# A held-back half tile of matrix products, cut into two chains of 256 columns around the end of a kernel

## The chip, the core and the metric

The kernel runs on one core of a Trainium2 chip. A core has a matrix engine (PE, whose weight loads the profile keeps apart as PEld), a vector engine (DVE), a scalar engine for activations and copies (ACT), a general engine (POOL) and a queue engine that issues transfers (SP). The metric is the device time of one execution in microseconds. Before the change it is 301.92 us, the median of three runs (301.86 to 302.01).

## The reference

```python
x: [16, 512, 1024]   w1, w2: [1024, 768]     # float32
y1 = np.matmul(x, w1)
y2 = np.matmul(x, w2)
return (np.tanh(y1) * y2).astype(np.float32)
```

Flattened, x has 8192 rows: 64 tiles of 128 rows. Each tile needs 768 columns of y1 and 768 of y2, over an inner length of 1024 (8 slices of 128).

## The kernel before

Inputs are cast to float16, sums are kept in float32. The 1536 columns of both weights are three blocks of 512: "a" (the first 512 of w1), "b" (the first 512 of w2) and "g" (the last 256 of w1 beside the last 256 of w2).

The first four row tiles (HEAD = 4) are "plain": for each block a chain of 8 matmuls adds up in one of the 8 PSUM banks (`plain`, `mm`, line 426), then ACT takes the tanh (`plain_tanh`, line 429) and DVE multiplies (`plain_mul`, line 433). The other 60 tiles go in 20 triples, numbered 0 to 19. A triple's 3x3 block product is computed by a fast scheme with 15 products p0 to p14 in place of 18: sums of x blocks (`x_sum`, line 417, DVE) times sums of weight blocks, each product 4 matmuls of 128x512 (`product`, line 442, PE), with copies of partial results (`c_copy`, line 446, ACT) and additions between banks (`c_add`, line 452, DVE). The list C_OPS names every step with what it needs. The steps that the change and the prediction touch are:

- p11, copy63, p0: p0 adds onto the bank of p11 after copy63 has read it.
- t0: the tanh of the bank that p0 finishes; add60: an addition that reads that bank and writes the bank in which p4 then continues; copy60 follows p4.
- p5, add52, seed16, p3: add52 changes the bank of p5, seed16 copies it into the bank that p2 continues, p3 then adds onto it.
- p3 is followed by th1 (a tanh of 256 columns, `c_tanh`, line 455) and add4, which both read the bank that p3 finishes; th0 reads what add4 writes.
- m0, m1, m2 (512 columns) and mh0, mh1, mh2 (256 columns) are the closing multiplications (`c_mul`, line 460).
- p14 needs the x sum S63, p13 needs S51 and add128; m2 needs p13, th2 and mh2 need p14.

A "flag" checks that the input magnitudes are in range: f1, f2, f3 (DVE, lines 463, 466, 470) add up what ACT has summed, f4 is a tiny matmul (line 473), f5 writes the flag (DVE, line 476). At the end every engine loads the flag (line 740) and branches to a general path when it is set; it is not.

Names carry the triple: p4.18 is p4 of the last but one triple, p4.19 of the last.

The order of all instructions is made at build time by `Planner`: each step has a cost per engine, a due time and needs; the planner lays them on the engines, gives each chain one of the 8 banks, and the instructions are then emitted in the order of the planned starts and stay in that order on each engine. The products have an order written out by hand (PE_ORDER; a "+" puts an entry into the next triple's round), with LAST_ORDER for the end of triple 19; the other steps follow from the planner.

One chain of the plain tiles is held back: block "g" of the fourth tile (mt = 3). Its 8 matmuls (m3g, `xT_kept` in the trace) are due at the very end and may start only behind p0.19, so that they fill PE where the last products wait. Its tanh (thg3), its multiplication (mug3) and its own store of 256 columns (st3M) close it.

A closing store (`store`, line 423) is issued by SP for each finished part. The last triple's three tiles are stored in two parts each: st59 and st58 are whole tiles of triple 18; st610/st611, st620/st621, st630/st631 are the 512 and the 256 columns of tiles 61 to 63. Every transfer that SP issues waits in SP's one queue of instructions.

Of the kernel before, what the change touches and what calls it, by code (L numbers as in the profile page):

```python
# [67 lines left out]

PE_ORDER = "7 0+ 13+ 6 10 4+ 5+ 9 12 1 14 3+ 2+ 11 8"
FIRST_ORDER = "7 1 10 6 12 9 11 8 14"  # L70
LAST_ORDER = "0 13 4 5 3 2"


class Planner:
# [9 lines left out]
    def op(self, name, engines, due, needs, fn, *args, behind=(), issued=(), chains=(), xfer=0.0, latency=None, seeds=False,  # L84
           lands=None, hold=0.0):
        assert name not in self.ops, name
        self.ops[name] = dict(engines=engines, due=due, needs=[n for n in needs if n], behind=[n for n in behind if n], issued=[n for n in issued if n], fn=fn, args=args,
                              chains=chains, xfer=xfer, latency=latency, seeds=seeds, lands=lands, hold=hold)
        for c in chains:
            self.chains.setdefault(c, {"left": 0, "bank": None, "end": 0.0})["left"] += 1  # L90
# [149 lines left out]
def kernel(  # L240
# [7 lines left out]
    nc = tc.nc  # L248
# [3 lines left out]
    KO = K // P  # L252
    KH = KO // 2
    MT = B * M // P
    F = 512
    G = N - F
    HEAD = 4
    TRIPLES = (MT - HEAD) // 3
# [29 lines left out]
    wh = once.tile([P, KO, 2 * N], f16, name="wh")  # L288
# [22 lines left out]
    pin = tc.keep_in_program_order  # L311
    engine = {"dve": nc.vector, "act": nc.scalar, "pool": nc.gpsimd, "sp": nc.sync}
    plan = Planner(8)
    op = plan.op

    def bank(chain):
        return banks[plan.chains[chain]["bank"]]

    BLOCK = {"a": 0, "g": F, "b": 2 * F}
    slices = [("a", k) for k in range(KO)] + [(s, k) for s in "gb" for k in (0, 4, 1, 5, 2, 6, 3, 7)]  # L320
# [5 lines left out]
    def w_cols(s, k):  # L326
        return wh[:, k, BLOCK[s]:BLOCK[s] + F]
# [4 lines left out]
    def xt(mt):  # L332
        return xt_kept if mt == HEAD - 1 else xt_bufs[mt % XT_BUFS]
# [89 lines left out]
        pin(nc.sync.dma_start(of[mt][:, lo:lo + n], out_tile(mt)[:, lo:lo + n]))  # L423

    def mm(e, chain, mt, k, rhs, first):
        pin(nc.tensor.matmul(bank(chain), xt(mt)[:, k, :], rhs, start=first, stop=k == KO - 1, skip_group_check=True))  # L426

    def plain_tanh(e, mt, lo, n, chain, at):
        pin(nc.scalar.activation(out_tile(mt)[:, lo:lo + n], bank(chain)[:, at:at + n], ACT.Tanh))
# [54 lines left out]
    MM = 0.2158  # L484
    SLOT = KH * MM
    CAST = {"a": {"dve": 0.37}, "g": {"act": 0.495}}
    FILL = {}
# [8 lines left out]
    for n, p in enumerate(FIRST_ORDER.split()):  # L496
        position["p" + p, 0] = 6 + n
    for n, p in enumerate(LAST_ORDER.split()):
        position["p" + p, TRIPLES - 1] = TRIPLES * 15 + n
    sequence = sorted((z, i, p) for (p, i), z in position.items())  # L500
    slot_of = {(i, p): ORIGIN + z * SLOT for z, i, p in sequence}
# [13 lines left out]
    for n, what in enumerate(on_sp):  # L515
# [3 lines left out]
        else:  # L519
            s, k = what[0], int(what[1])  # L520
# [3 lines left out]
               behind=[f"c{a}{b}" for a, b in old], lands=lands[what])  # L524
# [6 lines left out]
    landed = {}  # L531
# [32 lines left out]
    xt_readers = {mt: [] for mt in range(MT)}  # L564

    def plain(mt, s, due, behind=()):
        for n, k in enumerate([k for u, k in slices if u == s]):
            before = list(behind) + ([f"m{mt}{s}0"] if n else [])
            op(f"m{mt}{s}{k}", {"pe": MM}, due(n), [f"c{s}{k}", f"e{mt}{k // KH}"], mm, (s, mt), mt, k, w_cols(s, k), n == 0,
               behind=before, chains=[(s, mt)])  # L570
        last = [f"m{mt}{s}{k}" for k in range(KO)]
        xt_readers[mt] += last
        return last

    outs = {mt: [] for mt in range(MT)}

    def reuse_out(mt):
        return [f"st{mt - O_BUFS}"] if mt >= HEAD + O_BUFS else []

    def finals(mt, s, due, last):  # L580
        if s != "b":
            lo, n = (0, F) if s == "a" else (F, G)
            op(f"th{s}{mt}", {"act": 0.5 if n == F else 0.28}, due, last, plain_tanh, mt, lo, n, (s, mt), 0,
               behind=reuse_out(mt), chains=[(s, mt)])
        if s != "a":
            lo, n, at = (0, F, 0) if s == "b" else (F, G, G)
            op(f"mu{s}{mt}", {"dve": 0.6 if n == F else 0.33}, due, last + [f"th{'a' if s == 'b' else s}{mt}"], plain_mul, mt, lo, n,
               (s, mt), at, chains=[(s, mt)])
            outs[mt].insert(0 if s == "b" else 1, f"mu{s}{mt}")

    for n, s in enumerate("agb"):
        for mt in range(HEAD):
            if (s, mt) == ("g", HEAD - 1):
                due, behind = (lambda n: 1e4 + n), [f"p0.{TRIPLES - 1}"]
            else:
                due, behind = (lambda n: landed[slices["agb".index(s) * KO + n]] + 0.8 + 0.02 * mt), [FILL[mt]] if s == "b" and mt in FILL else []
            finals(mt, s, due(KO - 1) + (5.0, 3.0, 7.0)["agb".index(s)], plain(mt, s, due, behind))

    c_ops = {o[0]: o for o in C_OPS}
    readers = {}  # L600
# [44 lines left out]
    for i in range(TRIPLES):  # L645
# [3 lines left out]
        for v, a, b, how in A_SUMS:  # L649
            op(f"S{v}.{i}", {"dve": 0.335}, None, x_needs(i, a) + x_needs(i, b), x_sum, i, v, a, b, how,  # L650
               hold=needed(i, v) - S_AHEAD if i > 1 else 0.0,
               behind=[f"{r}.{i - S_BUFS}" for r in a_readers[v]] if i >= S_BUFS else first_done)
# [3 lines left out]
        for o in C_OPS:  # L656
            name, kind, needs = o[:3]
            needs = [f"{n}.{i}" for n in needs]
            chains = sorted({(i, p) for p in o[3:6] if isinstance(p, str) and p[0] == "c"})
# [16 lines left out]
            mt = HEAD + 3 * i + r  # L676
            due = soonest[i, name] + LAST
            if kind in ("t", "th"):
                lo, n = (0, F) if kind == "t" else (F, G)
                op(f"{name}.{i}", {"act": 0.5 if n == F else 0.285}, due, needs, c_tanh, i, r, o[4], lo, n, o[5],  # L680
                   behind=reuse_out(mt), chains=chains)
            else:
                lo, n, at = (0, F, 0) if kind == "m" else (F, G, G)
                op(f"{name}.{i}", {"dve": 0.6 if n == F else 0.335}, due + 1, needs, c_mul, i, r, o[4], lo, n, at, chains=chains)
                outs[mt].insert(0 if kind == "m" else 1, f"{name}.{i}")
    for mt in range(MT):
        i = (mt - HEAD) // 3 if mt >= HEAD else -1
        if mt < HEAD:
            n = F if mt == HEAD - 1 else N
# [11 lines left out]
    for mt in range(BY_PE, MT):  # L701
# [3 lines left out]
        if mt >= BY_PE + AHEAD:  # L705
# [4 lines left out]
           behind=xt_readers[mt - XT_BUFS] if mt >= XT_BUFS and mt - XT_BUFS != HEAD - 1 else [], xfer=1.2, latency=1.0 if mt < HEAD + 6 else 3.0)  # L710
# [128 lines left out]
```

## Time and profile before

| | us |
|---|---|
| median of three runs | 301.92 |
| the profiled execution | 302.25 |
| its span from the first to the last instruction | 300.4 |
| PE busy | 290.8 |
| DVE busy | 255.8 |
| ACT busy | 224.9 |
| mean granted TensorE clock | 0.997 |

The span is 1.85 us shorter than the profiled execution's own time, and that execution is 0.33 us above the median. In a row of the timeline the columns are start, length, engine, line, operation, what is written and read, the count, and in brackets the engine's idle time before it and what ended that. In a row of the chain of waits they are start, length and the piece of work that the end is traced back to. A matmul of 128x512 is shown with a length of 0.379 us, but they follow each other much closer, because they are pipelined.

### The profile page before, as it was taken

How to read it: one execution, taken by the hardware profiler on the slowest of the kernel's cores; microseconds unless marked ns; L12 is line 12 of the kernel's file. 1: busy time of each engine (PE TensorE's matmuls, PEld its weight loads, DVE VectorE, ACT ScalarE, POOL GpSimd, SP SyncE). 2: the span in 40 equal slices, each digit the busy share in tenths (PEclk: the TensorE clock that was granted, in tenths of full speed). 3: DMA queues.
4: the chain of work that ended last, by engine and by line, in shares of the span. 5: the costliest groups of instructions: out<-in, count | busy, mean ns of one | idle time of the engine just before them, and what ended most of it. 6: DMA issues, size and time to landing. Idle time of an engine off the chain costs nothing.

```text
span 300.4 us, 4674 instructions
## 1 busy us (share of the span) xinstructions
PE 290.8 (97%) x1377; PEld 132.8 (44%) x1377; DVE 255.8 (85%) x538; ACT 224.9 (75%) x451; POOL 52.5 (17%) x128
## 2 busy tenths in 40 slices
PE   8989999999999999999999999999999999999993
PEld 5434444444444444444444444444444444444441
DVE  1669999989889898988988898998988989897864
ACT  3577997597978879798697988758687786877443
POOL 0064044121220212112121221112022110000000
PEclk9999999999999999999999999999999999999998
DMA  6999999999999999999999999999999999231243
GB/s 232 386 294 196 170 188 188 189 207 241 302 195 249 216 264 283 257 267 216 252 172 212 182 234 176 246 214 244 227 204 205 172 242 260 97 136 52 107 158 125
DMA packets 84283, 63.51 MB, mean 211 GB/s; under 512 B 62752, under 2 KB 66336, under 8 KB 84256
## 3 DMA queue, kind: packets, MB, share of 16 engines
q1 hardware_dynamic: 73888, 45.36, 61.7%
q0 software_dynamic: 9792, 16.78, 36.2%
q10 hardware_dynamic: 576, 1.05, 1.0%
q8 instruction: 11, 0.18, 0.2%
q14 instruction: 16, 0.13, 0.1%
HBM read 39.85 MB, written 25.17 MB: 216 GB/s over the span
## 4 chain that ended last, share of the span: by engine, by line
PE 84%; DMA 7%; DVE 5%; issue 1%; ACT 1%; ACTq 0%; SPq 0%; POOL 0%; DVEq 0%
PE bank L442 80%; DMA arena<-in_w_dram 4%; PE bank L426 3%; DMA wh<-in_w_dram 2%; DMA xT<-xh 1%; DVE bank L452 1%; DVE o L460 1%; DVE early_x L417 1%; DVE arena L452 1%; ACT o L455 1%; PE bank L376 0%; ACTq L353 0%; DVE b L408 0%; ACT wh L362 0%; SPq L350 0%
## 5 line engine op out<-in xcount | busy, mean ns | idle before, releaser
L442 PE MATMUL bank<-b,early_x 128*128 128x512 f16 x640 | 148.4, 379 | 0.7 <-DVE arena L452 0.4
L442 PEld LDWEIGHTS <-early_x 128*128 128x128 f16 x800 | 78.2, 98 | 95.8 <-issue 2.1
L446 ACT ACTIVATE arena<-bank 128x512 f32<-128x512 f32 x100 | 59.0, 597 | 38.5 <-PE bank L442 37.5
L452 DVE TENSOR_TENSOR bank<-bank,arena 128x512 f32<-128x512 f32 x100 | 69.5, 695 | 19.1 <-ACT arena L446 13.2
L460 DVE TENSOR_TENSOR o<-o,bank 128x512 f32<-128x512 f32 (+1 forms) x120 | 61.1, 549 | 4.9 <-ACT o L455 3.2
L386 ACT ACTIVATE junk<-xh 128x1024 f16<-128x1024 f16 x60 | 63.1, 1051 | 0.1
L442 PEld LDWEIGHTS <-xT 128*128 128x128 f16 x400 | 38.9, 98 | 48.3 <-issue 1.4
L442 PE MATMUL bank<-b,xT 128*128 128x512 f16 x240 | 58.3, 379 | 0.0
L358 POOL DMA_DIRECT2D xh<-in_x_dram x60 | 31.7, 528 | 139.7 <-ACT junk L386 127.2
L455 ACT ACTIVATE o<-bank 128x256 f32<-128x256 f32 x80 | 33.0, 436 | 12.4 <-DVE bank L452 8.2
L442 PE MATMUL bank<-wh,xT 128*128 128x512 f16 x160 | 41.1, 379 | 0.6 <-DVE o L460 0.5
L442 PE MATMUL bank<-wh,early_x 128*128 128x512 f16 x160 | 41.1, 379 | 0.0
L417 DVE TENSOR_TENSOR early_x<-early_x,xT 128x512 f16<-128x512 f16 x80 | 32.3, 420 | 1.2 <-DMA xT<-xh 0.4
L455 ACT ACTIVATE o<-arena 128x512 f32<-128x512 f32 x40 | 25.0, 625 | 6.8 <-DVE arena L452 6.7
L446 ACT ACTIVATE bank<-bank 128x512 f32<-128x512 f32 x40 | 21.5, 570 | 1.9 <-DVE bank L452 1.1
L479 POOL CAST held<-xT 128x1 f32<-128x1 f16 x53 | 15.6, 295 | 39.5 <-DMA xT<-xh 39.4
L426 PE MATMUL bank<-wh,xT 128*128 128x512 f16 x72 | 19.1, 379 | 2.0 <-DMA wh<-in_w_dram 1.3
L417 DVE TENSOR_TENSOR early_x<-xT,xT 128x512 f16<-128x512 f16 x40 | 16.8, 419 | 0.0
L417 DVE TENSOR_TENSOR early_x<-xT,early_x 128x512 f16<-128x512 f16 x40 | 16.8, 419 | 0.0
L452 DVE TENSOR_TENSOR bank<-arena,bank 128x512 f32<-128x512 f32 x20 | 13.9, 696 | 2.4 <-ACT o L455 0.6
L452 DVE TENSOR_TENSOR arena<-arena,bank 128x512 f32<-128x512 f32 x20 | 13.6, 679 | 0.3 <-issue 0.3
L452 DVE TENSOR_TENSOR arena<-bank,arena 128x512 f32<-128x512 f32 x20 | 13.8, 688 | 0.0
(47 smaller groups left out, 134.3 us busy)
## 6 DMA issues: line engine op xcount, KB each, us to landing
out_dram<-o SPq DMA_DIRECT2D x60, 384.0 KB, 4.7
xh<-in_x_dram POOLq DMA_DIRECT2D x60, 256.0 KB, 5.6
arena<-in_w_dram SPq DMA_DIRECT2D x12, 256.0 KB, 5.5
early_x<-in_x_dram SPq DMA_DIRECT2D x8, 256.0 KB, 5.1
arena<-in_w_dram ACTq DMA_DIRECT2D x4, 256.0 KB, 5.8
wh<-in_w_dram POOLq DMA_DIRECT2D x8, 128.0 KB, 5.7
out_dram<-o SPq DMA_DIRECT2D x4, 256.0 KB, 3.0
xT<-xh SPq DMA_TRANSPOSE x57, 5.3
```

The costliest lines, as they stand in the source:

```text
L358: pin(nc.gpsimd.dma_start(xh(mt), xf[mt]))
L386: pin(nc.scalar.activation(junk[:, :src.shape[-1]], src, ACT.Abs, scale=scale, accum_out=sums[:, column:column + 1]))
L417: pin(engine[e].tensor_tensor(x_operand(i, v), x_operand(i, a), x_operand(i, b), OP[how]))
L426: pin(nc.tensor.matmul(bank(chain), xt(mt)[:, k, :], rhs, start=first, stop=k == KO - 1, skip_group_check=True))
L442: pin(nc.tensor.matmul(place(i, dst), x_operand(i, a)[:, k, :], w_rhs(b, k), start=begins and k == 0, stop=k == KH - 1, skip_group_check=T ...
L446: pin(nc.scalar.activation(place(i, dst), place(i, src), ACT.Copy, scale=float(sign)))
L452: pin(nc.vector.tensor_tensor(place(i, dst), a, b, ALU.add if signs == (1, 1) else ALU.subtract))
L455: pin(nc.scalar.activation(out_tile(HEAD + 3 * i + r)[:, lo:lo + n], place(i, src)[:, :n], ACT.Tanh, scale=float(sign)))
L460: pin(nc.vector.tensor_tensor(o, o, place(i, src)[:, at:at + n], ALU.mult))
L479: pin(nc.gpsimd.tensor_copy(held, xt(mt)[:, 0, :1]))
```

## The change

Three things are edited. LAST_ORDER now begins with p0, p14 and has p13 behind p5. The matmul helper writes only as many columns as its right side has. And the held-back chain m3g becomes two chains of 8 matmuls with 256 columns each: y0 (the w1 half, due right behind p0.19 as before) and y1 (the w2 half, behind p2.19, the last product). The tanh thg3 reads y0, the multiplication mug3 reads y1.

```diff
-LAST_ORDER = "0 13 4 5 3 2"
+LAST_ORDER = "0 14 4 5 13 3 2"
...
-        pin(nc.tensor.matmul(bank(chain), xt(mt)[:, k, :], rhs, start=first, stop=k == KO - 1, skip_group_check=True))
+        pin(nc.tensor.matmul(bank(chain)[:, :rhs.shape[-1]], xt(mt)[:, k, :], rhs, start=first, stop=k == KO - 1, skip_group_check=True))
...
             if (s, mt) == ("g", HEAD - 1):
-                due, behind = (lambda n: 1e4 + n), [f"p0.{TRIPLES - 1}"]
-            else:
-                due, behind = (lambda n: landed[slices["agb".index(s) * KO + n]] + 0.8 + 0.02 * mt), [FILL[mt]] if s == "b" and mt in FILL else []
+                continue
+            due, behind = (lambda n: landed[slices["agb".index(s) * KO + n]] + 0.8 + 0.02 * mt), [FILL[mt]] if s == "b" and mt in FILL else []
             finals(mt, s, due(KO - 1) + (5.0, 3.0, 7.0)["agb".index(s)], plain(mt, s, due, behind))
+
+    mt = HEAD - 1
+    ends = {}
+    for t, after in enumerate(("p0", "p2")):
+        chain = ("f", f"y{t}")
+        for n, k in enumerate(range(KO)):
+            op(f"m{mt}y{t}{k}", {"pe": MM / 2}, 1e4 * (1 + t) + n, [f"cg{k}", f"e{mt}{k // KH}"], mm, chain, mt, k,
+               wh[:, k, F + t * G:F + t * G + G], n == 0, behind=[f"m{mt}y{t}0" if n else f"{after}.{TRIPLES - 1}"], chains=[chain])
+        ends[t] = [f"m{mt}y{t}{k}" for k in range(KO)]
+        xt_readers[mt] += ends[t]
+    op(f"thg{mt}", {"act": 0.28}, slot_of[TRIPLES - 1, "p2"], ends[0], plain_tanh, mt, F, G, ("f", "y0"), 0, chains=[("f", "y0")])
+    op(f"mug{mt}", {"dve": 0.33}, 1e4, ends[1] + [f"thg{mt}"], plain_mul, mt, F, G, ("f", "y1"), 0, chains=[("f", "y1")])
+    outs[mt].append(f"mug{mt}")
```

What the planner makes of it shows in the two built programs. Up to p6.19 on PE they are the same, and what follows is, engine by engine:

```
PE before   p6.19 p10.19 p4.18 p5.18 f4 p9.19 p12.19 p1.19 p14.19 p3.18 p2.18 p11.19 p8.19 p0.19
            p13.19 g(1) p4.19 p5.19 g(7) p3.19 p2.19
PE after    p6.19 f4 p10.19 p4.18 p5.18 p9.19 p12.19 p1.19 p3.18 p2.18 p11.19 p8.19 p0.19
            p14.19 y0(1) p4.19 p5.19 p13.19 y0(7) p3.19 p2.19 y1(8)
DVE before  S35.19 f1 S63.19 add60.18 m0.18 m2.18 add312.19 f2 add64.19 S10.19 f3 S21.19 f5 add52.18 ...
            m0.19 m2.19 add52.19 add8.19 mug3 add4.19 mh1.19 m1.19 mh0.19
DVE after   S35.19 f1 f2 add60.18 f3 m0.18 m2.18 f5 add312.19 add64.19 S10.19 S21.19 add52.18 add8.18 S63.19 ...
            m0.19 mh2.19 add52.19 add8.19 m2.19 add4.19 mh1.19 m1.19 mh0.19 mug3
ACT before  ... copy56.19 t0.19 copy60.19 seed16.19 t1.19 thg3 th1.19 th0.19
ACT after   ... copy56.19 t0.19 th2.19 copy60.19 seed16.19 t1.19 thg3 th1.19 th0.19
SP before   st631 st59 st58 st610 st630 st3M st621 st620 st611
SP after    st59 st58 st610 st631 st630 st621 st620 st611 st3M
```

In the program before, th1.19 waits for p3.19, and add4.19 waits for th1.19. In the program after, add4.19 waits for p3.19, and th1.19 waits for add4.19. In both, add60 waits for t0.

## The prediction

> **What bounds the kernel now.** The page comes first (its engine table is in the section on the profile): PE is busy 97% of the span, so up to its last stretch the kernel is a stream of matmuls, and only what lengthens or shortens that stream counts. Then the chain of waits, from 260 us on, shows where the stream breaks and what follows it.
>
> ```profile
> span 300.4 us, 4674 instructions
> ```
> ```profile
> 281.00 0.17 PE bank L473
> ...
> 288.99 0.61 ACT o L455
> 289.60 0.02 issue
> 289.62 0.71 DVE bank L452
> 290.33 0.04 issue
> 290.38 1.89 PE bank L442 x8
> 292.26 1.51 PE bank L426 x7
> 293.77 1.00 PE bank L442 x4
> 294.78 0.02 issue
> 294.80 0.39 ACT o L455
> 295.19 0.02 issue
> 295.22 0.70 DVE bank L452
> 295.91 0.93 DVE o L460 x2
> ...
> 296.92 0.24 DVE o L460
> ```
>
> Read from the end: mh0.19 closes at 296.92 + 0.24 = 297.16. Before it on DVE stand m1.19 and mh1.19, then add4.19 (295.22), which waited for the tanh th1.19 (294.80), which waited for p3.19, whose start at 293.74 follows p5.19 and the two steps add52 and seed16. In front of p4.19 (290.38) lies another such loop: p0.19, t0 (288.99), add60 (289.62). And at 281.00 the chain passes through f4, the flag's tiny matmul.
>
> Next, the timeline of PE. Tile and weight names tell the products apart: at 278.99 p4.18 and p5.18, at 281.03 p9, p12, p1, at 283.61 p14, at 287.93 p0, at 288.79 p13, then one matmul of the held-back chain, at 290.38 p4 and p5, at 292.10 the other seven, at 293.74 p3 and p2.
>
> ```profile
> 278.99 1.89 PE L442 MATMUL bank<-b,early_x 128*128 128x512 f16 x8
> 281.03 2.75 PE L442 MATMUL bank<-b,early_x 128*128 128x512 f16 x12
> 283.61 1.03 PE L442 MATMUL bank<-wh,early_x 128*128 128x512 f16 x4
> ...
> 287.93 1.03 PE L442 MATMUL bank<-b,xT 128*128 128x512 f16 x4
> 288.79 1.03 PE L442 MATMUL bank<-wh,early_x 128*128 128x512 f16 x4
> 289.66 0.38 PE L426 MATMUL bank<-wh,xT_kept 128*128 128x512 f16 x1
> ...
> 292.10 1.67 PE L426 MATMUL bank<-wh,xT_kept 128*128 128x512 f16 x7
> 293.74 1.89 PE L442 MATMUL bank<-b,xT 128*128 128x512 f16 x8
> ```
>
> A product takes 288.79 - 287.93 = 0.86 us from start to start (0.863 over the three from 281.03 to 283.61 and on, less 0.01 at the first), a matmul 0.216, and the results of the last one appear 1.03 us after a product's start. Three stalls follow. p5.18 has issued at 278.99 + 2 x 0.863 = 280.72, and p9 starts at 281.03: 0.31 lost around f4. The first held-back matmul has issued at 289.88, p4 starts at 290.38: 0.50 lost to the loop through t0 and add60. Seven matmuls of 0.216 from 292.10 end at 293.61, p3 starts at 293.74: 0.13 lost to add52 and seed16.
>
> After DVE's end SP still has work: it issues the last stores, and the program ends 300.38 - 297.29 = 3.09 us after the last issue (the second of the two below: 296.86 + 0.81 - 0.38).
>
> ```profile
> 296.86 0.81 SPq L423 DMA_DIRECT2D out_dram<-o  x2
> ```
> ```profile
> L423 SPq DMA_DIRECT2D out_dram<-o x2: 333/358/382, 296.9 to 297.3; - x2
> ...
> DMA to landing us min/median/max: 1.9/2.0/2.0
> ```
>
> **The change, part by part.** *p14 moves behind p0.* One product leaves the stretch before p0: -0.86. All others there keep their order, and in the loop p11, copy63, p0 the same single product p8 lies between, so p0 can follow as closely as before. p14 comes back where PE waited for add60 in any case, in the place of p13.
>
> *The flag.* f1 to f3 have no due time of their own, and in the new DVE order f3 stands right behind add60.18, where it stood behind four more operations; f4 is put before p10.19.
>
> ```profile
> 277.23 0.70 DVE L452 TENSOR_TENSOR bank<-bank,arena 128x512 f32<-128x512 f32 x1 [0.69 <-ACT o L455]
> 277.84 1.28 DVE L460 TENSOR_TENSOR o<-o,bank 128x512 f32<-128x512 f32 x2
> ```
> ```profile
> 280.71 0.23 DVE L470 TENSOR_REDUCE count<-good 128x1 bf16<-128x80 f32 x1
> ```
>
> add60.18 starts at 277.23, waiting for t0.18, which the change does not touch; DVE's next operation starts at 277.84. That is now f3, done at 278.07. f4 started 0.06 after f3's end (280.94, 281.00), so it can start at 278.13. PE comes to that place when p6.19 has issued, which is p10.19's old start, 278.99 - 0.863 = 278.13. So f4 waits for next to nothing and costs the 0.03 that lie between it and the next matmul (281.00, 281.03). The 0.31 becomes 0.03: -0.28. What f3 puts off on DVE (m0.18, m2.18, add312, add64) moves by f3's own 0.23 at most, and by an estimate add312 and add64 end before 280.7; p9 and p12 want them at 280.75 and 281.61. If that cover is gone, PE waits for the difference. If f3 comes later after all, f4 waits as before. The bounds are 0 and -0.31; I take -0.28.
>
> p0 thus starts at 287.93 - 1.14 = 286.79.
>
> *The loop to p4* (p0, t0, add60) has no new member, so p4 starts at 290.38 - 1.14 = 289.24. The first matmul of y0 issues from 288.52 (p0 and p14 over) to 288.63; PE's stall is now 0.61, as the filler is half as wide. It costs nothing, because the loop and not PE sets p4. th2 moves to ACT behind t0 and ends long before copy60 is wanted.
>
> *The loop to p3* (p5, add52, seed16) lasted from p5's last issue, 290.38 + 1.73 = 292.11, to 293.74: 1.63. p5 now issues until 290.97, so p3 is due at 292.60. Under it lie p13 (0.86) and seven matmuls of 256 columns. The trace has 128x256 matmuls with a weight load each, the kernel's clock-keeping ones:
>
> ```profile
> 6.72 0.71 PE L340 MATMUL bank<-ones 128*128 128x256 bf16 x5
> 7.27 0.90 PE L426 MATMUL bank<-wh,xT 128*128 128x512 f16 x3
> ```
>
> Five take 7.27 - 6.72 = 0.55, so 0.11 each. These fetch the same weights each time, the new ones another slice, so the bounds are 0.11 and the 0.216 of a 512 one; I take 0.11, the same shape. 0.86 + 0.77 = 1.63: the fill is exactly as long as the loop, and p3 starts at 292.60.
>
> The Trainium skill ("TensorE: Matmul & The Clock Gate", section "LDWEIGHTS (loading the stationary operand)") puts a weight load at its columns over 1.2, an estimate of 107 ns here: were it not hidden, a 256-column matmul would cost as much as a 512 one, and the third rival's sum would hold. The trace's 0.11 for load and matmul together speaks for hiding.
>
> *th1 and add4 change places.* Both read p3's bank, and one now waits for the other the other way round. The previous rounds show this order too: the timelines of DVE and ACT have add4.17 and then th1.17 and th0.17.
>
> ```profile
> 272.42 0.70 DVE L452 TENSOR_TENSOR bank<-arena,bank 128x512 f32<-128x512 f32 x1
> ```
> ```profile
> 273.15 0.66 ACT L455 ACTIVATE o<-bank 128x256 f32<-128x256 f32 x2 [0.31 <-DVE bank L452]
> ```
>
> th1 started 0.03 after add4's end, so they do not overlap. Before, p3's end (294.78) to mh1's start was 0.02 + th1's 0.39 + 0.03 to add4, and 0.60 on from add4's start to mh1's. After, it is 0.03 + add4's whole 0.70 + 0.03 + 0.39 + 0.03 = 1.18 against 1.04: +0.14. p3 ends at 293.64, so mh1 starts at 294.82. Before, it was the first of
>
> ```profile
> 295.82 1.34 DVE L460 TENSOR_TENSOR o<-o,bank 128x256 f32<-128x256 f32 x3
> ```
>
> and so it is 1.00 earlier now. The three multiplications end at 296.16.
>
> *y1 and mug3.* y1 issues behind p2 from 292.60 + 1.73 = 294.33 to 295.21 and is done by 295.4. mug3 follows mh0 on DVE at 294.82 + 0.33 + 0.60 + 0.33 = 296.08 and ends at 296.5 (0.42 for 256 columns), so y1 has 0.7 of cover and costs nothing.
>
> *The stores.* m1 ended at 296.84 and its store was issued at 296.86; now it is 295.86. On SP the next issue follows after 0.81 - 0.38 = 0.43, DVE being done earlier. So mh0's store goes at 296.29 and st3M, now the last, at 296.72; DVE's 0.33 for mug3 hides behind SP's 0.43. Before, the last went at 297.29: -0.57. Its data have more ahead of them: after the 256 KB store, 256 KB instead of 128. At the rate of
>
> ```profile
> 298.00:299.00 1.00, 0.00 (x0) 0.00 (x0) 0.00 (x0) 0.00 (x0) 0.00 (x0) 0.78 0.79 281
> ```
>
> 131 KB take 0.47, so the last landing comes 0.43 - 0.47 = 0.04 later relative to its issue.
>
> **Sum:** -0.86 (p14) - 0.28 (f4) + 0.14 (th1 behind add4) + 0.43 (one more store behind) + 0.04 (landing) = -0.53. Against the profiled execution, 302.25 (its span of 300.4 and 1.85 around it), this is 301.72. That execution was 0.33 above the median, so in medians 301.92 - 0.53 = 301.4, 0.18% less.
>
> **The rivals.** *The flag keeps its stall.* If f3 or f4 is held up, up to 0.28 comes back: 301.7. For it speaks that f4 has no slack at all at 278.13; against it, that f3's only late input is add60.18, which the trace times.
>
> *The two readers of p3's bank do not wait for each other.* Then add4 starts at 293.67, mh1 0.61 later at 294.28, and the end gains another 0.54: 300.9. Against it stand rows 272.42 and 273.15 and the built program's wait.
>
> *Narrow matmuls as dear as wide ones (slower than before).* At 0.216 each, y0 puts p3 off by 7 x 0.106 = 0.74, and all behind it: -0.53 + 0.74 = +0.21, 302.1. It decides from 0.11 + 0.53/7 = 0.186 per matmul. Against it is the 0.55 for five.
>
> *A slow issue among the last stores (slower than before).* One of the nine last issues took 1.215:
>
> ```profile
> L423 SPq DMA_DIRECT2D out_dram<-o x9: 332/333/1215, 285.5 to 297.3; - x9
> ```
>
> Among the last three it would add 0.88: 302.3. It is the store of m2.19, the fifth from the end in both orders, where a long pause follows; that speaks against it. With the flag's stall on top it is 302.5 or more.
>
> **How the numbers follow.** A measurement of this kernel tells 0.2%, 0.6 us, from no change: the borders are 301.32 and 302.52. My forecast has 0.62, with a range of its own from 301.1 to 301.6, since the unknowns (f4's wait, SP's distances) are tenths; 0.28 of it lies below 301.32. The flag's stall has 0.15, the free readers 0.06, dear narrow matmuls 0.05, a slow issue 0.07, slow issue and stall together 0.05. Faster: 0.28 + 0.06 = 0.34. Slower: 0.05. Within 0.2%: 0.61. The range from 301.0 to 302.1 leaves out the free readers and the slow issues, 0.18 in all.
>
> **What would show it.** p9.19 starting near 280.75 and p0.19 near 286.79 would show the first two steps; a stall behind p6.19 would show the flag's. p3 near 292.60 and rows of seven narrow matmuls 0.77 apart show the fill; th1 starting at add4's end, and mh1 near 294.82, the swap; SP's last three issues 0.43 apart, near 296.72, the end. The prediction is wrong if the last issue comes before 296.5 or after 297.3, or if the span beyond it isn't 3.1.

## The result, and the profile after

| | runs | fastest us | median us | median above fastest |
|---|---|---|---|---|
| before | 22 | 301.56 | 302.73 | 1.17 |
| after | 22 | 300.97 | 301.29 | 0.32 |

The changed kernel is faster: the ratio of the times is 0.9958, with a 95% interval from 0.9946 to 0.9970, so 0.42% less time (0.30% to 0.54%). The time itself, 301.29, is 0.1 below the forecast; the gain is more than twice the forecast one, because the kernel before takes 302.73 as a rule and not the 301.92 of its first three runs. Between the two profiled executions it is near the forecast gain: 301.63 against 302.25, and the spans are 0.53 us apart (300.38 and 299.85).

The chain of waits of the changed kernel (start, length, piece of work):

```profile
278.29 0.01 PE bank L473
278.31 9.53 PE bank L442 x44
287.84 0.02 issue
287.86 0.61 ACT o L455
288.47 0.02 issue
288.49 0.71 DVE bank L452
289.20 0.04 issue
289.24 2.75 PE bank L442 x12
291.99 0.77 PE bank L426 x7
292.76 0.88 PE bank L442 x4
293.64 0.02 issue
293.67 0.71 DVE bank L452
294.37 0.02 issue
294.40 0.39 ACT o L455
294.79 0.02 issue
294.81 0.04 DVE o L460
...
296.09 0.41 DVE o L433
```

Between 278.31 and p0.19's end there is no gap any more: f4 takes 0.01 on the chain, where DVE's steps and f4 broke it at 281.00 before. p4 starts at 289.24. From there PE is busy without a gap through p4, p5, p13 (x12), the seven narrow matmuls and p3. Then add4 (293.67) runs before th1 (294.40), and mh1 follows th1 at 294.81. mug3 (line 433) now stands at the very end, at 296.09.

The timeline of PE of the same kernel:

```profile
277.27 1.03 PE L442 MATMUL bank<-b,early_x 128*128 128x512 f16 x4
278.13 0.18 PE L473 MATMUL bank<-count,ones 128*128 128x8 bf16 x1
278.17 1.02 PE L442 MATMUL bank<-wh,xT 128*128 128x512 f16 x4
279.03 4.48 PE L442 MATMUL bank<-b,early_x 128*128 128x512 f16 x20
...
286.80 1.03 PE L442 MATMUL bank<-b,xT 128*128 128x512 f16 x4
...
291.83 0.93 PE L426 MATMUL bank<-wh,xT_kept 128*128 128x256 f16 x7
292.60 1.89 PE L442 MATMUL bank<-b,xT 128*128 128x512 f16 x8
294.33 1.04 PE L426 MATMUL bank<-wh,xT_kept 128*128 128x256 f16 x8
```

p6.19 starts at 277.27 as before, f4 directly behind it, and p0.19 at 286.80 (287.93 before). Seven narrow matmuls lie between 291.83 and 292.60: 0.11 each. On DVE, f3 stands where the built order had put it, 0.60 behind add60.18:

```profile
277.24 0.70 DVE L452 TENSOR_TENSOR bank<-bank,arena 128x512 f32<-128x512 f32 x1 [0.74 <-ACT o L455]
277.84 0.23 DVE L470 TENSOR_REDUCE count<-good 128x1 bf16<-128x80 f32 x1
```

And the last three issues on SP, with the lengths of the last four:

```profile
295.86 1.30 SPq L423 DMA_DIRECT2D out_dram<-o  x3
```
```profile
L423 SPq DMA_DIRECT2D out_dram<-o x4: 332/358/400, 295.3 to 296.8; - x4
```

The last one starts at 295.86 + 1.30 - 0.40 = 296.76, 0.53 earlier than before (297.29).

### The profile page after: what moved, and what is told of

Same layout as the page of the kernel before. It is cut to its first block, busy times and chain, and to the rows that moved or that the text cites. A ratio compares the mean times of both kernels' runs of the same rounds, so it can differ in the third digit from the quotient of the medians.

```text
span 299.9 us, 4690 instructions
## 1 busy us (share of the span) xinstructions
PE 291.0 (97%) x1385; PEld 133.8 (45%) x1385; DVE 255.9 (85%) x538; ACT 224.9 (75%) x451; POOL 49.8 (17%) x128
## 4 chain that ended last, share of the span: by engine, by line
PE 85%; DMA 7%; DVE 4%; issue 1%; ACT 1%; ACTq 0%; SPq 0%; POOL 0%; DVEq 0%
PE bank L442 82%; DMA arena<-in_w_dram 4%; PE bank L426 3%; DMA wh<-in_w_dram 2%; DMA xT<-xh 1%; DVE bank L452 1%; DVE early_x L417 1%; DVE o L460 1%; PE bank L376 0%; DVE arena L452 0%; ACTq L353 0%; DVE b L408 0%; ACT o L455 0%; ACT wh L362 0%; SPq L350 0%
## 5 line engine op out<-in xcount | busy, mean ns | idle before, releaser
L455 ACT ACTIVATE o<-bank 128x256 f32<-128x256 f32 (+1 forms) x80 | 32.9, 436 | 11.2 <-DVE bank L452 7.7
L479 POOL CAST held<-xT 128x1 f32<-128x1 f16 x53 | 12.6, 239 | 103.7 <-DMA xT<-xh 103.7
```

Source lines behind the costliest of these rows:

```text
L455: pin(nc.scalar.activation(out_tile(HEAD + 3 * i + r)[:, lo:lo + n], place(i, src)[:, :n], ACT.Tanh, scale=float(sign)))
L479: pin(nc.gpsimd.tensor_copy(held, xt(mt)[:, 0, :1]))
```

## The experiments

All were timed beside the kernel before, the edits of the changed kernel too; medians set against the changed kernel's 301.29 are from different times. Single executions differ by some tenths in when the stream of products settles, at about 41 us: the same matmul starts at 40.75 in the first profile of the kernel before, at 40.50 and 40.27 in its two other profiles. From there to p6.19 the stream keeps its distances in these three. So places near the end are compared by their distance from p6.19 or f4. Two questions are put: are the steps of the sum right, one by one, and where does the rest of the measured gain come from, given that the profiled executions are only the forecast 0.5 us apart?

### The kernel before once more

No edit.

> The kernel before once more, unchanged, timed against itself. Theory (the change gains only in the last 25 us, 0.53 us, and whatever the medians show beyond that is how far single runs of the kernel before lie apart): ratio 1.000 within 0.002, single runs between 301.5 and 304 us, span of the profile 300.4 us, p9.19 starting at 281.03 and the last store issued at 297.29. Rival (the kernel before loses a further 0.7 us in most runs at a place after 278 us that the first profile did not catch): the same ratio, but the profile shows a stall of 0.5 us or more in that stretch which the first profile does not have.

Measured: ratio 1.0001 (0.9985 to 1.0017), twelve runs from 301.62 to 303.65 with a median of 302.44; the 29 other runs of the kernel before beside them have a median of 302.51. So the kernel before spreads over 2 us on this chip. The profile is an execution of 301.90 us with a span of 300.1, whose stream of products came 0.26 earlier (p6.19 at 277.00 for 277.26) and ran on as the first one; it has no stall that the first lacks. The rival's stall is not in it, but it is a short execution, so this alone doesn't decide.

### The flag moved alone

```diff
-    op("f2", {"dve": 0.2}, None, ["f1"], flag_2)
-    op("f3", {"dve": 0.2}, None, ["f2"], flag_3)
+    op("f2", {"dve": 0.2}, 274.0, ["f1"], flag_2, hold=274.0)
+    op("f3", {"dve": 0.2}, 274.0, ["f2"], flag_3, hold=275.0)
...
-               hold=needed(i, v) - S_AHEAD if i > 1 else 0.0,
+               hold=max(needed(i, v) - S_AHEAD, 278.5 if (v, i) == (63, TRIPLES - 1) else 0.0) if i > 1 else 0.0,
```

With f1 held to 273.8 in the same way, the planner gives f1, f2, add60.18, f3 on DVE and f4 before p10.19; PE, ACT and SP keep all else.

> The kernel before with the flag's steps alone moved: f2 and f3 around add60.18, f4 before p10.19, as in the changed kernel; products, held-back chain and stores as before. Theory: f4 costs 0.03 us in place of 0.31, so p9.19 starts at 280.75, p0.19 at 287.65 and the last store is issued at 297.01; span 300.1 us, time 0.28 us (0.09%) below the kernel before. Rival (the flag's place costs the kernel before more in most runs than in the profiled one, and is where most of the measured 1.3 us comes from): time 0.8 us or more (0.27%) below.

Measured: ratio 0.9992 (0.9974 to 1.0010). The chain of waits of this kernel:

```profile
278.31 10.39 PE bank L442 x48
288.70 0.02 issue
288.73 0.61 ACT o L455
289.33 0.02 issue
289.36 0.71 DVE bank L452
290.07 0.04 issue
290.11 1.89 PE bank L442 x8
```

t0 starts at 288.73 where the kernel before has 288.99, p4 at 290.11 for 290.38: 0.27 gained. The last store is issued at 297.02 (297.01 expected). The median fell by 0.35, and the fastest run by 0.24. The runs still spread, from 301.42 to 303.26. In the profile the flag step is right in size; the interval of the ratio holds both this gain and none. The rest of the gain isn't made there.

### The flag put back in the changed kernel

```diff
-    op("f2", {"dve": 0.2}, None, ["f1"], flag_2)
-    op("f3", {"dve": 0.2}, None, ["f2"], flag_3)
+    op("f2", {"dve": 0.2}, None, ["f1"], flag_2, hold=276.6)
+    op("f3", {"dve": 0.2}, None, ["f2"], flag_3, hold=277.9)
```

> The changed kernel with the flag's steps put back where the kernel before has them (f2 behind add312.19, f3 behind S10.19, f4 behind p5.18). Theory: f4 stalls PE for 0.31 us again, p9.19 starts at 281.03, all behind it 0.28 us later than in the changed kernel: p0.19 at 287.08, last store at 297.04, span 300.1 us, 0.25 us below the kernel before. Rival (the flag is where most of the gain comes from): no more than 0.1 us below the kernel before, or the time of the changed kernel plus 0.8 us.

Measured: ratio 0.9963 (0.9941 to 0.9985), twelve runs from 301.32 to 302.36, median 301.55: 0.26 above the changed kernel, as the theory had it. In its profile f3 and f4 are back on the chain, and with p6.19 at 277.03 the last store is issued at 296.79, which is 0.27 later than in the changed kernel by the distance from p6.19:

```profile
280.56 0.16 DVE count L470
280.72 0.04 issue
280.76 0.17 PE bank L473
```

Its 301.55 is no "0.25 below the kernel before" in medians but 0.96 below (302.51). So most of the gain stays when the flag's step is taken away, and it goes with short spread: median less fastest run is 0.23 here and 0.74 with the flag moved alone.

### th1 ahead of add4

```diff
+                if (name, i) == ("add4", TRIPLES - 1):
+                    before = before + [f"th1.{i}"]
...
+                   behind=[f"mh1.{i}"] if (name, i) == ("m1", TRIPLES - 1) else [])
```

The second edit keeps m1 behind mh1 on DVE, so that only the wait between the two readers turns round.

> The changed kernel with th1.19 ahead of add4.19 again, as in the kernel before; all else in the same order. Theory: mh1.19 starts 0.14 us earlier (294.68 in place of 294.82), the last store is issued at 296.62, span 299.7 us, 0.14 us below the changed kernel and 0.67 us (0.22%) below the kernel before. Rival (the order of the two readers is hidden behind y1 or the stores): the span stays at 299.9 us.

Measured: ratio 0.9951 (0.9931 to 0.9970), six runs from 300.94 to 301.26, median 301.07. The chain of waits of this kernel:

```profile
292.45 0.88 PE bank L442 x4
293.33 0.02 issue
293.35 0.39 ACT o L455
293.75 0.02 issue
293.77 0.70 DVE bank L452
```

th1 runs first and add4 waits for it. f4 stands at 277.82 here, 0.31 before its place in the changed kernel, and the last store is issued at 296.32, so 296.63 on the same footing: 0.13 gained, of the 0.14 that the sum had charged.

> The changed kernel with th1.19 ahead of add4.19 once more, for the interval: ratio 0.995 to 0.9965 against the kernel before, runs between 300.9 and 301.7 us, median 0.1 to 0.3 us below the changed kernel's 301.29. If its first six runs were lucky, the median comes to 301.3 or more.

Measured: ratio 0.9958 (0.9946 to 0.9970), eleven runs from 300.88 to 301.40, median 301.14. Two medians 0.22 and 0.15 below the changed kernel's, measured at other times than its own, fit the 0.13 of the profile; no interval between the two was measured. It has the lowest median found, and was faster than the kernel before both times.

### The order of the products alone

```diff
-LAST_ORDER = "0 13 4 5 3 2"
+LAST_ORDER = "0 14 4 5 13 3 2"
```

> The kernel before with LAST_ORDER alone changed: the held-back chain stays one chain of 512 columns, of which the planner puts five matmuls ahead of p3 and three behind p2. Theory: the steps as in the changed kernel, but p3 starts 0.10 us later (four wide matmuls and p13 under the loop, 1.73 for 1.63), so the last store is issued 0.10 us later than in the changed kernel, at 296.82, span 299.9 to 300.0 us, fastest runs 0.43 us below the kernel before. By the program read it has as many PE instructions as the kernel before, so its runs should spread over 1.5 us; by the rival (spread comes from the order) they should lie together as the changed kernel's do.

Measured: ratio 0.9956 (0.9939 to 0.9972), seven runs from 301.08 to 301.75, median 301.37. f4 stands 0.29 earlier than in the changed kernel and the last store is issued at 296.56, so 296.85 on its footing (296.82 expected, 0.09 behind the changed kernel). One line of the diff thus gives almost all of the gain, the flag's earlier place included (f4 at 277.84), since the planner moves f4 with it; the split of the chain gives the last 0.1. On the spread the expectation missed: this kernel has as many PE instructions as the kernel before, and its runs lie together (median less fastest 0.29).

### The split alone

```diff
-LAST_ORDER = "0 14 4 5 13 3 2"
+LAST_ORDER = "0 13 4 5 3 2"
```

on the changed kernel.

> The changed kernel with LAST_ORDER as before: only the held-back chain is split. Theory: p0 and p4 start as in the kernel before (287.93, 290.38), PE idles 0.86 us in place of 0.13 ahead of p3, which still starts at 293.74; th1 behind add4 costs 0.14 and the store of mug3 at the end 0.43, so the last store is issued at 297.86, span 300.9 us, fastest runs 0.57 us above the kernel before. Its PE program is 16 instructions longer, so its runs should lie within 0.8 us by the program read; by the rival they should spread as the kernel before's.

Measured: ratio 0.9996 (0.9983 to 1.0009), twelve runs from 301.92 to 303.02. Its chain of waits has the idle stretch ahead of p3 (add52, then seed16 on ACT, then PE):

```profile
292.60 0.71 DVE bank L452
293.31 0.02 issue
293.33 0.59 ACT bank L446
293.92 0.04 issue
293.96 1.04 PE bank L442 x4
```

Its f4 stands 0.23 later than in the kernel before (281.23 for 281.00), and the last store is issued at 298.12: 297.89 on the same footing, 0.60 later (0.57 expected). The fastest run is 0.27 above the fastest of the kernel before beside it (301.65), less than the 0.60 of the profile, and the median only 0.08 above (302.62 for 302.54). So in the profile the split alone costs, and it pays there only because the new order puts p13 under the loop to p3, where the narrow y0 then just fits; the run times do not show this cost, and why is open. The runs spread more than expected (median less fastest 0.70). The profiled run, 303.02, is the longest of the twelve, though none of its last three store issues took more than 0.40. What it has is a late stream, behind a wait for a transposing load of x:

```profile
40.99 1.04 PE L442 MATMUL bank<-wh,xT 128*128 128x512 f16 x4 [0.48 <-DMA xT<-xh]
```

So part of the spread between runs is made near the start of the kernel.

### A program read that meets the last stores

The page counts 11 transfers of PE's own program, 16 KB each (q8, of kind "instruction", 0.18 MB; they come about every 250 recorded PE instructions, the first after 204, the last after 2726 of 2769, and are taken for PE's for that reason). In the trace of the kernel before the last one starts at 291.3, and the one store issued meanwhile is the slow one of the prediction's last row (1.215). In the two other profiles of that kernel it starts at 295.1 and 294.8. In the changed kernel it starts at 290.18, just ahead of the store issued at 290.23, which took 1.67. So a store issued while the program is read can be held up, and in the kernel before the read lies near the last stores in some executions. That became the second theory. (In the three profiled executions of the unchanged kernel no issue among the last three took over 0.42, and their times, 302.25, 301.90 and 301.70, follow f4: 281.00, 280.74, 280.52.)

```diff
-    for n in range(WARM):
+    for n in range(WARM - 2):
...
+    for n in range(10):
+        pin(nc.tensor.matmul(banks[n % 8][:, :8], ones.bitcast(bf16)[:, :P], ones.bitcast(bf16)[:, :8], start=True, stop=True))
```

> The kernel before with 16 more PE instructions at its very start (the 14 opening matmuls of 256 columns become 12, and 10 of 8 columns follow, each with its weight load), as many as the change adds at the end; nothing else moves. Theory (one of the 16 KB reads of PE's program falls near the last stores in many runs of the kernel before; a store issued during such a read takes 1.2 to 1.8 us to issue in place of 0.33; 16 more instructions bring the read forward by 8 matmuls' worth of program): the read starts near 291 us in the profile, the single runs lie together within 0.8 us but for a few, and the median falls by 0.6 us (ratio 0.998) although the last store is issued at the same 297.3. Rival (the spread of the kernel before comes from its order of stores or products): spread and median as before, ratio 1.000.

Measured: ratio 1.0005 (0.9990 to 1.0020), twelve runs from 302.19 to 303.52 and one of 305.82, the profiled one; the median rose by 0.13. This expectation failed: the read didn't come earlier, and the median didn't fall. The profile still shows the collision itself. That execution's f4 stands 2.39 us late (283.39), of which 1.18 was lost at a wait for a transposing load and 0.94 behind a copy on ACT, both in the middle of the kernel:

```profile
159.42 1.04 PE L442 MATMUL bank<-wh,xT 128*128 128x512 f16 x4 [1.01 <-DMA xT<-xh]
```
```profile
169.01 1.02 PE L442 MATMUL bank<-wh,early_x 128*128 128x512 f16 x4 [0.78 <-ACT bank L446]
```

So its span says nothing of the edit; its last stores were

```profile
298.65 2.40 SPq L423 DMA_DIRECT2D out_dram<-o  x3
```
```profile
L423 SPq DMA_DIRECT2D out_dram<-o x9: 332/333/1372, 287.9 to 299.7; - x9
```

with the read from 299.18 to 300.67: the last issue, at 299.67, took 1.37 in place of 0.38. The one before it, at 299.25, took 0.33 although the read had begun.

The counterpart takes 16 PE instructions away from the start of the changed kernel:

```diff
-    for n in range(WARM):
-        pin(nc.tensor.matmul(banks[n % 8][:, n // 8 % 2 * 2 * P:][:, :2 * P], ones.bitcast(bf16)[:, :P], ones.bitcast(bf16), start=True, stop=True))
+    for n in range(WARM // 2):
+        pin(nc.tensor.matmul(banks[n], ones.bitcast(bf16)[:, :P], ones.bitcast(bf16)[:, None, :].to_broadcast([P, 2, 2 * P]), start=True, stop=True))
```

(and one matmul of 512 columns in place of two of 256 in the first later group).

> The changed kernel with 16 PE instructions fewer at its very start (7 opening matmuls of 512 columns in place of 14 of 256, and one of 512 in place of two of 256 later); the rest as in the changed kernel. Theory (the place of the program read): the read starts at 293 to 296 us in part of the runs, the runs spread over 1.5 us or more, and the median rises by 0.5 us or more over the changed kernel's, to 301.8 to 302.2. Rival (the changed order is steady by itself): runs within 301.0 to 302.2 with a median near 301.3, as the changed kernel.

Measured: ratio 0.9975 (0.9960 to 0.9991), twelve runs from 300.76 to 303.03, median 301.82, which is 0.53 above the changed kernel. In its profile the stretch from f4 to the last issue is as long as in the changed kernel (18.63), but the read lies at the end, from 296.17 to 297.30:

```profile
L426 SPq DMA_DIRECT2D out_dram<-o x4: 332/358/1042, 294.9 to 296.4; - x4
```

The last issue took 1.04 in place of the changed kernel's 0.40, and the execution 302.14 us. Nothing near the end was edited, so the order of the products and stores alone does not make the runs steady. The two ratios' intervals just overlap (0.9960 to 0.9970); the spread, 1.06 against 0.32, is the clearer sign. The edit does change the start, though (f4 stands 0.35 earlier), and whether the start varies more for it was not measured.

Then the read was moved far away, by 80 PE instructions in the middle of the kernel before:

```diff
     def product(e, i, dst, a, b, begins):
+        if dst == "c4" and i in (3, 6, 9, 12):
+            for n in range(10):
+                pin(nc.tensor.matmul(place(i, dst)[:, :8], ones.bitcast(bf16)[:, :P], ones.bitcast(bf16)[:, :8], start=True, stop=True))
```

> The kernel before with 80 more PE instructions in the middle: ten matmuls of 8 columns with their weight loads ahead of p7 in triples 3, 6, 9 and 12, whose results p7 overwrites. They cost PE at most 0.1 us each, 2 to 4 us in all, which is not the question. Theory (PE's last 16 KB program read comes where its records number some 2720 to 2760; in the kernel before that is 0 to 6 us before the end of its 2769, so that it meets the last stores in part of the runs): with 2849 records the read falls 10 us or more before the end and cannot meet the last stores, so median minus fastest run falls from 0.85 us to 0.4 us or less. Rival (the spread is made at the start of the kernel or by the order of its products): median minus fastest run stays at 0.7 us or more.

Measured: twelve runs from 302.42 to 303.26, median 302.73, ratio 1.0013 (1.0002 to 1.0024). The read starts at 282.9, and no issue near the end is long:

```profile
L423 SPq DMA_DIRECT2D out_dram<-o x9: 332/333/384, 286.1 to 297.8; - x9
```

The forty matmuls cost 1.0 in the profile, not 2 to 4: each ten take 0.26 (67.15 - 66.89), four times.

```profile
66.89 0.39 PE L443 MATMUL bank<-ones 128*128 128x8 bf16 x10
67.15 1.02 PE L445 MATMUL bank<-wh,xT 128*128 128x512 f16 x4
```

That f4 stands only 0.51 later than in the first profile (281.51 for 281.00) comes from a stream that settled early, at 40.29 for 40.75. Median less fastest run is 0.31, for 1.14 of the kernel before beside it (301.50, 302.64), as the theory had it. Less 1.0 the median is 301.7, 0.9 below the kernel before's, and the fastest run 301.4, 0.1 below its fastest.

Then the three last stores were issued by ACT:

```diff
-        pin(nc.sync.dma_start(of[mt][:, lo:lo + n], out_tile(mt)[:, lo:lo + n]))
+        queue = nc.scalar if (mt, lo) in ((MT - 2, 0), (MT - 2, F), (MT - 3, F)) else nc.sync
+        pin(queue.dma_start(of[mt][:, lo:lo + n], out_tile(mt)[:, lo:lo + n]))
```

> The kernel before with its last three stores (of mh1, m1, mh0) issued by ACT in place of SP; all orders the same. Theory (a store issued by SP while PE's program is read takes up to 1.8 us to issue): if ACT's issue is held up in the same way, the spread stays (median minus fastest run 0.7 us or more) and a profile with the read near 295 to 297 us shows an issue on ACT of 1 us or more; if ACT's issue is free of it, median minus fastest run falls to 0.4 us. Fastest runs within 0.2 us of the kernel before's in either case, as the landing sets the end. Rival (no such collision matters): spread as before with no long issue anywhere in the profile.

Measured: ratio 1.0011 (0.9998 to 1.0025), twelve runs from 302.23 to 303.15. The spread is smaller (median less fastest 0.50), between the two values that the expectation had named, and the fastest run is 0.7 slower than that of the kernel before, against the expectation; in the profile the last issue is only 0.12 later (297.40 for 297.29), so the rest of that is not explained. The run tells nothing for or against. In its profile the read started at 295.3 and was over before ACT's first store, so whether ACT's issue would be held up is open.

Last, the kernel before was profiled once more, without an edit.

> One more profile of the kernel before, unchanged. Theory (PE's last program read meets the last stores in part of its runs): either the read starts before 295 us and the execution takes 301.5 to 302.3 us, or it starts between 295 and 298 us, one of the last three issues takes 0.8 us or more, and the execution takes 302.5 us or more. Rival (no such collision in this kernel): an execution of 302.5 us or more in which all of the last three issues take under 0.45 us and the excess lies elsewhere.

Measured: 301.70 us, with the read from 294.83 to 295.83 and the issue at 295.78 held up to 0.42, the others short. It is the first of the theory's two cases. An execution of the unchanged kernel of 302.5 us or more was never the profiled one.

Side by side:

| kernel | runs | median less fastest us | last program read starts (profile) |
|---|---|---|---|
| before (first comparison) | 22 | 1.17 | 291.3; 295.1 and 294.8 in other profiles |
| flag moved alone | 12 | 0.74 | 294.9 |
| split alone | 12 | 0.70 | 291.7 |
| changed less 16 instructions | 12 | 1.06 | 296.2 |
| before and 16 instructions | 13 | 0.48 | 299.2 |
| before, last stores on ACT | 12 | 0.50 | 295.3 |
| changed | 22 | 0.32 | 290.2 |
| changed, flag back | 12 | 0.23 | 290.2 |
| changed, th1 first | 6 | 0.13 | 290.0 |
| changed, th1 first, again | 11 | 0.26 | 289.9 |
| order alone | 7 | 0.29 | 289.9 |
| before and 80 instructions | 12 | 0.31 | 282.9 |

Where the profile has the read at 290.2 or earlier, the spread is 0.13 to 0.32; where it has it later, 0.48 to 1.17. The contrast depends on the measure. The middle half of the runs lies within 1.13 for the kernel before and 0.18 with 80 instructions more, but within 0.59 for the changed kernel and 0.43, 0.41 and 0.51 for the split alone, the stores on ACT and the 16 instructions less. And the reads come from one or a few profiles each, the spreads from other runs.

## Why the prediction was right, and where it fell short

*p14 behind p0, -0.86, and the flag, -0.28.* Right: p0.19 at 286.80 (286.79 forecast). The flag alone gave 0.27 in the profile of the kernel before, and taking it back cost 0.27 in that of the changed kernel.

*The loops to p4 and p3.* Right: 289.24 and 292.60, to 0.01. Narrow matmuls cost 0.11 with a fresh weight load each, the lower bound that was taken; the rival in which they are as dear as wide ones is out.

*th1 behind add4, +0.14.* Right in mechanism and size: th1 starts 0.03 behind add4's end, which rules out the rival of free readers, and undone, the step gives back 0.13.

*One more store, +0.43, and the landing, +0.04.* mug3 ended at 296.50 (296.5), the last store was issued at 296.76 (296.72), because the issue before it took 0.38 and not 0.33. The 0.04 for the landing did not come: the span beyond the last issue is 3.09 in both kernels. The two errors of 0.04 cancel, so that the span fell by the forecast 0.53; this exactness is luck.

*The sum, -0.53.* The profiled last issue moved by 0.53, the fastest runs by 0.59 (301.56 to 300.97).

*From the sum to the medians.* This is the step that fell short: "in medians 301.92 - 0.53". It took the three runs shown for what the kernel before takes as a rule, and a profile of 302.25 for an execution a little long. Its median over 22 runs is 302.73, and its runs lie 1.17 above the fastest in the median, the changed kernel's only 0.32. The difference, 0.85, and the 0.59 between the fastest make up the 1.44 between the medians. The row that told of the cause was quoted, the one issue of 1.215, but only as a rival that would harm the changed kernel; the prediction put the change's risk there and didn't ask what it costs the kernel before. So the likeliest class, within 0.2%, was wrong, and faster, at 0.34, came true. That the time itself came within 0.1 of the forecast is in part luck: the three runs that it starts from lie 0.8 below the kernel's median, and the change took away about as much beyond its forecast gain.

How far the cause is shown: the forecast gain is shown step by step, by the profiles and by the flag, th1 and order edits. That an issue takes 1.0 to 1.4 us when the read meets it at the end is shown in two edited kernels, and it costs the execution: from the last issue to the end of the execution it is 5.74 and 6.15 there, against 4.86 to 4.96 in the twelve other profiles. That the spread goes when the read is moved away, and comes back where the read is found at the end with the tail untouched, is seen in one kernel each; both edits change more than the read. The 80 instructions leave four breaks of 0.26 in the stream, and the profile with 16 instructions more shows that PE can lose 2.1 us in the middle, so a kernel that catches up in such breaks is a rival that was not tested. Single runs of 305.5 to 307.4 occur with both kernels and are not explained. That the long executions of the unchanged kernel are such collisions is argued from this, since none of them was profiled; part of the spread is made near the start of the kernel. What sets the start of the read remains open: the same program has it at 291.3 and at 295.1, 16 instructions more did not bring it forward, and the new order alone, without one instruction more, did. In the four profiles in which it lies at the end without a long issue it starts within 0.1 us of PE's last matmul; in the two with the long issue it starts some 1.5 us behind it.

## What to carry to other kernels

Where a stream of matmuls waits for a loop through other engines, count which products lie under the loop and which ahead of it: moving one product (0.86 us) from ahead of a loop to under it, one line of the diff, gave nearly the whole gain here, with the flag's earlier place that came along; the narrow chain only trimmed what stuck out. An expected gain of half a microsecond should be set against the spread of single runs of both kernels before it is called too small to tell: a change can also take away a random loss that the one profile does not hold. And two readers of one bank are worth ordering by hand, by which of the two has the longer work behind it.

## What the runs showed of the hardware

A store issue on SP that takes 0.33 us can take 1.0 to 1.8 us when it falls into a 16 KB read of PE's program (1.04, 1.37 and, well before the end, 1.22 to 1.84). Not every issue in a read suffers: with the split alone the store issued at 291.76, 0.09 into the read, took 0.33, and in the first run with th1 ahead the read at 290.0 began while a store was being issued, and that one took 0.38. But such stores land later: the one at 291.76 landed after 3.0 us, where the store in its place takes 2.1 in the last profile of the kernel before, and the two issued at 289.5 and 289.9 with the new order alone landed after 3.3 to 3.4, where the two in their places take 2.0 in the changed kernel with 16 instructions less.
